# A scheduler's clock with other matmul costs, and a margin before side matmuls, in a two-layer hybrid trunk

## The chip, the cores and the metric

The kernel runs on one core of a Trainium2 chip. The metric is the device time of one execution in microseconds; the time before is the median of three runs. The engines are named as in the profile: PE (TensorE, its weight loads apart as PEld), DVE (VectorE), ACT (ScalarE), POOL (GpSimd) and SP (SyncE).

## The reference, cut to what matters

256 tokens of width 1024 pass two layers. All products are computed in float32 accuracy.

```python
for l in range(2):
    x = x + 0.5 * swiglu_ffn(rms_norm(x, ffn1_norm[l]), ...)        # 1024 -> 2 x 2816 -> 1024
    h = rms_norm(x, mix_norm[l])
    rg_x, rg_g, sb_q, sb_k, sb_v, c_q, c_kv, k_r, gate_logits = jnp.split(h @ w_in[l], ...)
    y_a = rg_lru(causal_depthwise_conv(rg_x, ...), ...) * jax.nn.gelu(rg_g)
    y_b = stick_breaking_attention(sb_q, sb_k, sb_v)                # 8 heads of 128
    y_c = mla_branch(c_q, c_kv, k_r, ...)                           # 8 heads, latents of 256
    g_a, g_b, g_c = jnp.split(jax.nn.sigmoid(gate_logits), 3, axis=-1)
    merged = g_a * (y_a @ w_branch_a[l]) + g_b * (y_b @ w_branch_b[l]) + g_c * (y_c @ w_branch_c[l])
    x = x + merged @ w_out[l]
    x = x + 0.5 * swiglu_ffn(rms_norm(x, ffn2_norm[l]), ...)
return rms_norm(x, final_norm)
```

## The kernel before

The activations stay in SBUF, transposed (features on the partitions). All weights are read once, as one stream of sub-blocks of 128 x 512 floats in the order in which they are used. Each float32 value, of a weight or of an activation, is split into two float32r parts: ACT casts the high part, DVE subtracts it to get the low part. Weights are split in pieces of 1024 columns (`split_to`, line 409), two pieces ahead of their use (tiles `raw`, `hi`, `lo`). A product is then three float32r products. In a feature group (`feature_group`, line 509: 256 features of all tokens) each k-tile of 128 rows gives four matmuls, for each of two blocks one of 512 columns against `hi` and one of 256 columns against `lo`. In a token group (`token_group`, line 530) a k-tile gives six of 512 columns. These groups are the **main stream**. Their sums are in two PSUM tiles `acc`, for short or last groups in `side` tiles, of which there are four.

Between the two feed-forward blocks of a layer stands the mixer, whose groups come in the order `MIX_ORDER` (line 31). What is not a large product there is **side work**: generators that take up a group's result (`evac`), the stick-breaking attention (`stick_pair`, line 907), the recurrence with its gate matmuls (`rg_chain`, line 830, which reads `r` tiles made by ACT and DVE), latent attention (`mla_pair`, line 1061), norms (`squares`, line 612, and `broadcast`, line 642). A group that needs a result of side work asks for it when it comes to that k-tile (`Pairs`, line 1128), and `drain` (line 313) then emits what is missing, whether it fits or not. The branch products ask in this way: `brb` for stick-breaking attention, `bra` for the recurrence, `brc` for latent attention, two k-tiles for each pair of heads.

All engines run their instructions in program order. The order is decided when the program is built, by a model clock (`Clock`, line 120): for each engine the time until which it is held, and for each tile when it was written and read and by which engine. Each instruction is an `Op` (line 156) with a cost in ns by its engine and shape (lines 172 to 186): a DVE operation of n columns costs 68 + 1.042 n as a rule, an ACT operation 95 + 0.833 n, and a matmul 2.5 + 0.4167 n with n at least 256, four times the columns for float32 operands. The clock has no term for one engine's work slowing another's. `Op.emit` (line 191) books the instruction and calls the engine at line 197, so that nearly every instruction stands at L197 in the profile.

Main-stream instructions are emitted at once. After each k-tile of a group, `tick` (line 295) goes through the running tasks and emits the operations at the head of each for as long as `fits` (line 262) allows. For DVE and ACT an operation may start at most 50 ns (500 for urgent tasks, which are those that take up results) after the later of its engine's clock and PE's, and unless urgent must end within 1800 ns of PE's clock. For PE these lines decide, in which `s` is the earliest start by the clock, with 130 ns after a write by another engine:

```python
        if op.e == "pe":
            if s > c.t["pe"] + 60:
                return False
            if not t["urgent"]:
                if self.side <= 0:
                    return False
                self.side -= op.cost
            return True
```

`side` is set to 350 ns at each tick. A task's operations are emitted in its own order, so one that is refused holds back those behind it in its task, and no other task's.

Of the kernel before, what the change touches and what calls it, by code (L numbers as in the profile page):

```python
# [6 lines left out]
F32 = mybir.dt.float32  # L7
# [16 lines left out]
# columns of the packed per-layer vectors  # L24
# [12 lines left out]
# of each group of columns: the matrix, the first column, the k-tiles  # L37
# [9 lines left out]
def group_stream(what, n):  # L47
    """Sub-blocks of [128, 512]: one k-tile of 512 columns, or two k-tiles of 256."""
    if what == "ckv":
        for k in range(0, 9, 3):  # L50
            yield ("ckv0", "in", k, C_C + 256)
            yield ("ckv1", "in", k, C_C + 256)
    elif what in TOKENS:
        m, c, nk = TOKENS[what]
        for k in range(nk):
            yield ("one", m, k, c + 512 * n)
    elif what in FEATURES:
        m, c, nk = FEATURES[what]
        for k in range(0, nk, 2):
            yield ("two", m, k, c + 256 * n)  # L60
    else:
        for k in range(0, KD, 2):
            yield ("gu", what, k, 128 * n)


def layer_stream(l):
    """Order in which a layer's weight sub-blocks of [128, 512] are read."""
    for f in (1, 2):
        if f == 2:
            for g in MIX_ORDER:  # L70
                yield from group_stream(*g)
        for n in range(KF):
            yield from group_stream(f"gu{f}", n)
        if (l, f) == (L - 1, 2):
            for n in range(2):
                yield from group_stream("last", n)
        else:
            for n in range(4):
                yield from group_stream(f"dn{f}", n)
# [10 lines left out]
class Slots:  # L90
    """Tiles handed out in the order in which they were given back."""
# [17 lines left out]
# for each function the tables to load for it; a table holds all functions that name it  # L109
# [10 lines left out]
class Clock:  # L120
    """Estimated times (ns): until when each engine is held by what has been emitted, and
    when each tile's contents are there and have been read."""
# [33 lines left out]
class Op:  # L156
    """An instruction to be emitted, with what it costs by the clock."""

    def __init__(self, engine, name, op, args, kw):
        self.f, self.e, self.args, self.kw = getattr(engine, op), name, args, kw  # L160
        self.engine = engine
        out = kw.get("out", args[0] if args else None)
        n = 1
        for d in out.shape[1:]:
            n *= d
        outs = [out] + ([kw["accum_out"]] if kw.get("accum_out") is not None else [])
        aps = [x for x in (*args, *kw.values()) if hasattr(x, "tensor")]
        self.outs = {x.tensor.name for x in outs}
        self.ins = {x.tensor.name for x in aps if all(x is not o for o in outs)}
        self.table, self.tail = None, 80  # L170
        if op == "dma_start":
            self.cost, self.tail = 50, 2500
        elif name == "pe":
            self.tail = 165
            wide = op == "matmul" and args[2].dtype == F32
            self.cost = 2.5 + 0.4167 * (4 * n if wide else max(n, 256))
        elif name == "act":
            self.table = TABLES.get(kw.get("func"))
            extra = sum(90 for k in ("scale", "bias") if not isinstance(kw.get(k, 0.0), (int, float)))
            self.cost = 95 + extra + 0.833 * n  # L180
        elif name == "dve":
            fast = op in ("tensor_scalar", "tensor_copy") and all(x.space != bass.MemoryType.PSUM for x in aps)
            rate = {"reciprocal": 6.5, "tensor_tensor_scan": 2.1}.get(op, 0.55 if fast else 1.042)
            self.cost = 68 + rate * n
        else:
            self.cost = 150 + (166 if kw.get("op") == ALU.pow else 2.1) * n

# [12 lines left out]
class Timed:  # L200
    """An engine whose instructions are emitted at once from the main stream, and left to
    the scheduler from side work."""
# [15 lines left out]
class Tasks:  # L218
    """Side work: generators whose instructions are emitted, each generator's in order, where
    the clock says that they hold up no engine. What follows a yield runs after what came  # L220
    before it has been emitted."""
# [8 lines left out]
    SIDE = 350  # L230

# [30 lines left out]
    def fits(self, op, t):  # L262
        c = self.clock
        if op.e in ("pool", "sp"):
            return True
        s = op.when(c)
        if op.e == "pe":
            if s > c.t["pe"] + 60:
                return False
            if not t["urgent"]:  # L270
                if self.side <= 0:
                    return False
                self.side -= op.cost
            return True
        if s > max(c.t[op.e], c.t["pe"]) + t["early"]:
            return False
        return t["urgent"] or s + op.cost <= c.t["pe"] + self.LIMIT

    def advance(self, t, force=False):
        """Emits what it can of a task; whether there was any."""  # L280
# [32 lines left out]
    def drain(self, *tasks, done=None):  # L313
        """Emits the given tasks, whether they fit or not, to their end or until `done`."""
# [19 lines left out]
def trunk(tc, xT_in, pos_in, w_in, rgw_in, fin_in, const_in, out):  # L334
# [4 lines left out]
    with ctx:  # L339
# [18 lines left out]
        # x^T, two k-tiles of [128, 256] in each  # L358
# [4 lines left out]
        # [hi | lo] of two k-tiles  # L363
# [27 lines left out]
        def load(out, in_):  # L391
            """One of the first loads: they come one after the other."""
            nc.sync.dma_start(out=out, in_=in_)  # L393
            n = 4 * 128
            for d in out.shape[1:]:
                n *= d
            arrival[0] += max(n / 360, 475)
            clock.written[out.tensor.name] = (arrival[0] + 950, "dma")
# [56 lines left out]
        def both(ap):  # L455
            """[128, 256] as [128, 2, 256]"""
            return ap.rearrange("p (j t) -> p j t", j=1).to_broadcast([128, 2, 256])

        def hilo(src, hl, j=None, g=1.0):
            """src [128, 2, 256], or k-tile j of it, in two float32r parts."""  # L460
# [39 lines left out]
        def parts(a):  # L500
            """What of [128, 2, ...] each tile of a's holds."""
# [7 lines left out]
        def feature_group(kts, evac, last=0):  # L509
            """256 features of all tokens: the two halves of a bank are summed by `evac`. The  # L510
            last steps run block by block."""
# [18 lines left out]
        def token_group(kts, evac, last=0):  # L530
            """512 features, tokens on the partitions."""
# [15 lines left out]
        def narrow_group(kts, width, weights, evac):  # L547
            """The same with [128, width] weights, as (hi, lo) from `weights`."""
# [9 lines left out]
        def features(a):  # L558
            """What a feature group made, to SBUF."""
# [8 lines left out]
        def scaled(a, src, key, extra=None):  # L568
            """The same, times a scale per token."""
# [13 lines left out]
        def transpose_pair(srcs, o):  # L583
            """Two [128, 128] blocks from column o of every token tile, to [128, 2, 256]."""
# [18 lines left out]
        def first_norm(nm, n):  # L603
            """K-tiles 2n and 2n+1 of x are final: their two parts, and squares."""
# [37 lines left out]
        def broadcast(b, r, dst, key, start=False):  # L642
            """Columns r [128, NT], to a row of them on every partition."""
# [10 lines left out]
        class Lazy:  # L654
            """The k-tiles of x^T, each pair asked for when it is needed."""
# [113 lines left out]
        def gen_scaled(a, scales):  # L769
            """PSUM [tok, 512] times a per-token scale, to SBUF; alternating engines."""  # L770
# [40 lines left out]
        def rg_g(mx, p):  # L811
            def gelu(x):
                """x (1 + tanh(c (x + 0.044715 x^3))): twice the gelu."""
# [16 lines left out]
        def rg_chain(mx, ps):  # L830
            """Gates, recurrence and output gate of the channel pairs ps (256 channels each)."""
            vo = mx["v"]
            # with y = -log(a): a = exp(-y), 1 - a^2 = T (1 + a)^2, T = tanh(y / 2)
# [59 lines left out]
        def head_T(mx, key, p, r, extra=None):  # L893
            """Two heads, transposed."""
# [12 lines left out]
        def stick_pair(mx, p):  # L907
# [8 lines left out]
            for j in range(2):  # L916
# [9 lines left out]
                # log(1 + exp(z)) = max(z, 0) + log(1 + exp(-|z|))  # L926
# [72 lines left out]
        def rope(e, dst, src, tmp, nh, t):  # L999
            """dst = src rotated; all [128, nh, 64], tmp [128, nh, 64]."""  # L1000
# [40 lines left out]
        def k_rope(mx, f):  # L1041
            """[tok, 64] in columns t * 256 of f, to [64, tok] on both halves of the partitions,
            with zeros in place of the other half."""
# [84 lines left out]
        class Pairs:  # L1128
            """K-tiles that side work makes, two at a time."""
# [12 lines left out]
        def mix(nm, ntasks, nxt, l):  # L1142
# [37 lines left out]
            def many(work, width):  # L1180
                """Up to `width` at a time, each of them a task that can be waited for."""
# [12 lines left out]
            def gate(b, n):  # L1194
                def sigmoid(f):
                    """1 + tanh(x / 2): twice the sigmoid."""
# [10 lines left out]
            def branch(i, b, n):  # L1207
                """The i-th of the branches."""
# [108 lines left out]
        def tables():  # L1317
            """cos and sin of the positions' angles, and 4 softplus(-lambda)."""
# [144 lines left out]
```

## Time and profile before

| | us |
|---|---|
| median of three runs | 1467.37 |
| lowest and highest run | 1466.5, 1467.78 |
| span of the profiled execution | 1467.2 |
| PE busy | 1442.0 |
| PEld busy | 1261.0 |
| DVE busy | 1115.6 |
| ACT busy | 894.3 |
| POOL busy | 146.1 |

For the profiled execution the page gives its span, from the first to the last instruction; no other time of that execution is recorded, so sums are made against the span. Busy times are unions of the records of an engine. The ends of matmuls are modelled and overlap with the next, so PE's true pace is read from the starts of successive matmuls. In the names, numbers of buffers are left out: `acc<-r,hi` is a main matmul from an activation part and a high weight part, `side<-r,r` a gate matmul, `side<-f,f` a matmul of attention, `side<-f,cst` of 256 columns the broadcast of a norm.

### The profile page before, as it was taken

Reading aid. Unit: us, or ns where it says so; the run is one execution under the profiler, and the core shown is the slowest. Engines: PE = TensorE matmul, PEld = TensorE weight load, DVE = VectorE, ACT = ScalarE, POOL = GpSimd, SP = SyncE. Lnnn points to the kernel's source line nnn. Section 1 sums busy time; section 2 is a strip of 40 time slices with the busy share of each in tenths; the row PEclk is TensorE's granted clock in tenths of the full one; section 3 lists DMA queues with packets and bytes.
Section 4 is the critical chain, followed back from the end, with each engine's and each line's share of the span. In section 5 each row is a group of like instructions: output and inputs, shape, how many; then the busy total and the mean of one; then the engine's idle time right before and its main releaser. Section 6 shows DMA issues by size and latency. Waiting matters only on the chain.

```text
span 1467.2 us, 20804 instructions
## 1 busy us (share of the span) xinstructions
PE 1442.0 (98%) x8248; PEld 1261.0 (86%) x8248; DVE 1115.6 (76%) x1548; ACT 894.3 (61%) x1372; POOL 146.1 (10%) x120
## 2 busy tenths in 40 slices
PE   6999999999999999999999999999999999999998
PEld 5888888888888888888888888898888888888886
DVE  6878567689987788877677766676989877877853
ACT  4665446888665656665455554478885655566643
POOL 3000001123310000000000000111334000100001
PEclk9999999999999999999999999999999999999999
DMA  6555555534543455555545554544445434555452
GB/s 215 199 201 177 197 180 180 179 134 153 182 171 144 145 199 176 197 188 187 200 172 189 184 200 173 187 174 149 151 156 189 169 122 173 195 190 196 179 199 86
DMA packets 38081, 258.15 MB, mean 176 GB/s; under 512 B 4320, under 2 KB 4960, under 8 KB 7520
## 3 DMA queue, kind: packets, MB, share of 16 engines
q1 hardware_dynamic: 37152, 254.21, 48.5%
q0 software_dynamic: 832, 2.62, 0.6%
q8 instruction: 64, 1.05, 0.3%
q14 instruction: 33, 0.27, 0.1%
HBM read 255.77 MB, written 1.05 MB: 175 GB/s over the span
## 4 chain that ended last, share of the span: by engine, by line
PE 92%; DVE 5%; issue 1%; ACT 1%; DMA 0%; SPq 0%; POOLq 0%; POOL 0%; DVEq 0%; ACTq 0%
PE acc L197 77%; PE side L197 15%; DVE lo L197 2%; DVE f L197 2%; DVE r L197 1%; DMA x<-xT 0%; ACT hi L197 0%; ACT f L197 0%; SPq L393 0%; ACT r L197 0%; POOLq L1459 0%; POOL rms L197 0%; DVE rms L197 0%; DVEq L197 0%; ACTq L197 0%
## 5 line engine op out<-in xcount | busy, mean ns | idle before, releaser
L197 PE MATMUL acc<-r,hi 128*128 128x512 f32 x3148 | 1135.1, 403 | 9.4 <-ACT hi L197 5.5
L197 PE MATMUL acc<-r,lo 128*128 128x256 f32 x3148 | 882.7, 280 | 2.1 <-DVE lo L197 2.1
L197 DVE TENSOR_TENSOR lo<-raw,hi 128x1024 fp32r<-128x1024 f32 (+2 forms) x485 | 596.4, 1232 | 235.7 <-ACT hi L197 234.2
L197 PEld LDWEIGHTS acc<-r,hi 128*128 128x128 f32 x3148 | 593.0, 188 | 141.0 <-ACT hi L197 5.5
L197 PEld LDWEIGHTS acc<-r,lo 128*128 128x128 f32 x3148 | 596.7, 190 | 5.6 <-DVE lo L197 3.1
L197 ACT CAST hi<-raw 128x1024 fp32r<-128x1024 f32 (+2 forms) x485 | 501.5, 1040 | 137.3 <-PE acc L197 95.0
L197 POOL TENSOR_TENSOR f<-f,f 128x512 f32<-128x512 f32 (+1 forms) x51 | 89.1, 1753 | 1039.8 <-ACT f L197 955.8
L197 ACT COPY f<-acc 128x512 f32<-128x512 f32 x166 | 97.4, 587 | 126.7 <-PE acc L197 122.9
L197 ACT ACTIVATE f<-f 128x256 f32<-128x256 f32 (+3 forms) x190 | 94.9, 502 | 84.5 <-DVE f L197 83.3
L197 DVE TENSOR_TENSOR f<-acc,f 128x512 f32<-128x512 f32 x166 | 113.8, 685 | 39.1 <-ACT f L197 38.5
L197 DVE TENSOR_TENSOR f<-f,f 128x512 f32<-128x512 f32 x179 | 126.3, 706 | 8.8 <-ACT f L197 2.6
L197 PE MATMUL acc<-hi,r 128*128 128x512 f32 (+2 forms) x344 | 96.9, 358 | 0.0
L197 ACT CAST r<-f 128x256 fp32r<-128x256 f32 (+2 forms) x130 | 58.6, 455 | 61.1 <-DVE f L197 59.8
L197 PE MATMUL side<-r,hi 128*128 128x512 f32 x260 | 92.0, 395 | 0.0
L197 PE MATMUL side<-r,lo 128*128 128x256 f32 x260 | 72.6, 279 | 0.0
L197 PE MATMUL side<-f,f 128*128 128x256 f32 (+1 forms) x320 | 71.6, 327 | 0.0
L197 PEld LDWEIGHTS acc<-hi,r 128*128 128x128 f32 x344 | 61.6, 189 | 8.4
L197 DVE TENSOR_TENSOR r<-f,r 128x256 fp32r<-128x256 f32 (+2 forms) x130 | 64.7, 502 | 2.0 <-ACT r L197 1.9
L197 PE MATMUL acc<-lo,r 128*128 128x512 f32 (+2 forms) x172 | 61.1, 355 | 0.0
L197 PEld LDWEIGHTS side<-r,hi 128*128 128x128 f32 x260 | 48.7, 187 | 11.1
L197 PEld LDWEIGHTS side<-f,f 128*128 128x128 f32 x320 | 45.8, 190 | 4.9
L197 PEld LDWEIGHTS side<-r,lo 128*128 128x128 f32 x260 | 49.1, 189 | 0.0
(89 smaller groups left out, 806.2 us busy)
## 6 DMA issues: line engine op xcount, KB each, us to landing
raw<-w SPq DMA_DIRECT2D x238, 1024.0 KB, 4.8
f<-rgw POOLq DMA_DIRECT2D x8, 256.0 KB, 3.4
raw<-w SPq DMA_DIRECT2D x7, 256.0 KB, 6.9
out<-f SPq DMA_DIRECT2D x4, 256.0 KB, 2.2
x<-xT SPq DMA_DIRECT2D x3, 256.0 KB, 6.7
f<-fin POOLq DMA_DIRECT2D x2, 256.0 KB, 3.7
cst<-const SPq DMA_DIRECT2D x1, 336.0 KB, 5.5
x<-xT SPq DMA_DIRECT2D x2, 128.0 KB, 2.5
```

The costliest lines, as they stand in the source:

```text
L197: return self.f(*self.args, **self.kw)
```

## The change

It does two things. The cost of a PE instruction comes from a new function, `streamed`, which tells transposes, float32, float32r and the rest apart. And a PE operation of side work (or of a norm) is let in only where the modelled end of each operand that another engine wrote lies at least `LATE` = 900 ns before PE's clock. `drain` and forced emission do not ask `fits` and are as before. Everything else in the diff takes out comments.

```diff
@@ class Op
         elif name == "pe":
             self.tail = 165
-            wide = op == "matmul" and args[2].dtype == F32
-            self.cost = 2.5 + 0.4167 * (4 * n if wide else max(n, 256))
+            self.cost = self.streamed(op, args[2].dtype if op == "matmul" else F32, n)
...
+    @staticmethod
+    def streamed(op, dtype, n):
+
+        if op == "transpose":
+            return max(109, 0.852 * n)
+        if dtype == F32:
+            return 2 * max(112, 0.852 * n)
+        if dtype == F32R:
+            return 13.5 + 0.4167 * max(n, 256)
+        return 30 + 0.4167 * n
+
+    def settled(self, c):
+
+        return max((c.written[n][0] for n in self.ins if n in c.written and c.written[n][1] != self.e), default=0.0)
+
@@ class Tasks
     SIDE = 350
+
+    LATE = 900
...
         if op.e == "pe":
             if s > c.t["pe"] + 60:
                 return False
+            if op.settled(c) + self.LATE > c.t["pe"]:
+                return False
             if not t["urgent"]:
```

## Rows read from the trace of the kernel before

**Rows 1.** The page, part 1: busy time of each engine, its share, instructions.
```profile
PE 1442.0 (98%) x8248; PEld 1261.0 (86%) x8248; DVE 1115.6 (76%) x1548; ACT 894.3 (61%) x1372; POOL 146.1 (10%) x120
```
**Rows 2.** The page, part 2: the granted clock of PE in 40 slices.
```profile
PEclk9999999999999999999999999999999999999999
```
**Rows 3.** The chain that ended last: start, length, engine, tile, count.
```profile
31.97 155.31 PE acc L197 x896
...
499.26 25.66 PE acc L197 x148
```
**Rows 4.** Windows: length, then busy time of each engine with its instructions.
```profile
0.00:32.00 32.00, 20.53 (x83) 16.58 (x84) 18.80 (x27) 13.47 (x23) 11.21 (x13) 1.00 0.67 234
1062.00:1068.00 6.00, 3.66 (x23) 3.19 (x24) 6.00 (x8) 5.32 (x9) 3.11 (x3) 1.00 0.44 138
```
**Rows 5.** All waits of PE: total us, times, longest.
```profile
PE acc L197 <- ACT hi L197: 5.5, 1, 5.5
PE side L197 <- DVE r L197: 4.7, 4, 1.5
PE acc L197 <- DVE r L197: 3.9, 1, 3.9
PE acc L197 <- DVE lo L197: 2.1, 2, 1.9
PE side L197 <- DVE f L197: 1.9, 2, 0.9
```
**Rows 6.** Timeline of PE, layer 0: start, length, instruction, and idle before.
```profile
339.22 0.36 PE L197 MATMUL side<-r,r 128*128 128x256 f32 x1
340.48 0.38 PE L197 MATMUL side<-r,r 128*128 128x256 f32 x1 [0.90 <-DVE r L197]
...
341.40 0.65 PE L197 MATMUL side<-r,r 128*128 128x256 f32 x4
341.88 0.40 PE L197 MATMUL acc<-r,hi 128*128 128x512 f32 x1
...
342.57 0.28 PE L197 MATMUL side<-r,r 128*128 128x256 f32 x1
344.32 0.62 PE L197 MATMUL side<-r,r 128*128 128x256 f32 x3 [1.47 <-DVE r L197]
...
406.89 0.28 PE L197 MATMUL acc<-r,lo 128*128 128x256 f32 x1
408.10 0.70 PE L197 MATMUL side<-f,cst 128*128 128x256 f32 x2 [0.93 <-DVE f L197]
```
**Rows 7.** Timelines of DVE and of POOL at these places.
```profile
340.35 1.63 DVE L197 TENSOR_TENSOR lo<-raw,hi 128x1024 fp32r<-128x1024 f32 x1
341.90 2.37 DVE L197 TENSOR_TENSOR r<-f,r 128x512 fp32r<-128x512 f32 x2
...
406.21 1.83 DVE L197 TENSOR_SCALAR f<-cst,rc 128x128 f32<-128x128 f32 x2
...
340.99 2.13 POOL L197 TENSOR_TENSOR f<-f,f 128x512 f32<-128x512 f32 x1
...
405.15 2.28 POOL L197 TENSOR_TENSOR f<-f,f 128x512 f32<-128x512 f32 x1
```
**Rows 8.** Windows as in rows 4; the third busy time is that of DVE.
```profile
310.00:320.00 10.00, 10.00 (x64) 8.96 (x63) 9.96 (x17) 8.70 (x16) 3.24 (x3) 1.00 0.44 141
...
340.00:350.00 10.00, 8.05 (x50) 7.13 (x51) 9.97 (x10) 6.80 (x12) 7.49 (x5) 1.00 0.32 107
```
**Rows 9.** Timelines: a split on DVE, and PE's first matmul on its result.
```profile
294.81 1.23 DVE L197 TENSOR_TENSOR lo<-raw,hi 128x1024 fp32r<-128x1024 f32 x1 [3.33 <-ACT hi L197]
...
296.80 0.28 PE L197 MATMUL acc<-r,lo 128*128 128x256 f32 x1
```
**Rows 10.** Timelines: the last attention matmul of layer 0, and a result's two parts.
```profile
498.87 0.38 PE L197 MATMUL side<-f,f 128*128 128x128 f32 x2
...
340.32 0.58 ACT L197 CAST r<-side 128x512 fp32r<-128x512 f32 x1
...
344.19 0.68 DVE L197 TENSOR_TENSOR r<-side,r 128x512 fp32r<-128x512 f32 x1
```

## The prediction

> **What bounds the kernel now.** I read the busy shares first: PE is busy 1442.0 us of a span of 1467.2, DVE 76% and ACT 61% [rows 1]. The slices say that this holds in every stretch, and that the granted clock is at full speed nearly throughout [rows 2]. Since matmuls overlap in such records, I checked the stream by start-to-start times: in the first feed-forward 896 matmuls take 155.31 us with no gap, 0.347 us per pair of one 512- and one 256-column matmul [rows 3]. So the kernel is a dense stream of matmuls, and only two things could shorten it without removing a matmul: the head, where PE is busy 20.53 of the first 32 us [rows 4], and the few places where PE waits. The change adds, removes and resizes no instruction; it only reorders. The whole prize is therefore in the list of PE's waits [rows 5]. Its three entries at `acc` belong to the head, before the side work of the mixers; those at `side` are 4.7 + 1.9 = 6.6 us.
>
> The timeline shows these six: three in each layer, at the same places, so I work them out in layer 0 and double. The gate matmuls of `rg_chain` (`side<-r,r`) stand 0.12 us apart when nothing is late (four in 0.48 us); one stands 1.26 us after its forerunner and another 1.75: stalls of 1.14 and 1.63 us. The broadcast of the latent norm (`side<-f,cst`) starts 1.21 us after a 256-column matmul that takes 0.12: a stall of 1.09 [rows 6]. That is 3.86 us per layer, **7.7 us in all** (6.6 as the wait view counts it, which starts from modelled ends). A window of layer 1 shows the same hole: 3.66 us busy of 6.00 [rows 4].
>
> **Why PE waits there.** In program order PE runs everything in turn, so a side matmul put in too early holds up the whole stream behind it. The clock thought that the operand was there; DVE was late. Behind 340 us two `r<-f,r` took 2.37 us together where the clock has 0.60 for each (68 + 1.042 x 512 ns), and a `lo` split took 1.63 where it has 1.14, while POOL ran a 2.13 us tensor_tensor; before the broadcast, two DVE operations of 128 columns took 1.83 us, beside a POOL operation of 2.28 us [rows 7]. The clock knows nothing of this; nothing in its costs couples POOL with DVE.
>
> **The change, part by part.** (1) *The margin.* So far a side matmul was let in when its operand's modelled time plus 130 was at most PE's clock plus 60, that is 70 ns behind it. Now 900 ns are wanted: 830 more. Side work is tried once per tick, every four matmuls or 0.69 us in a feature group, so an operation slips by one tick or two (0.69 or 1.39), 0.83 on average. If DVE's lag stays as it is, the isolated stall of 1.09 falls by 0.83. The two gate stalls are one lag of 1.14 + 1.63 = 2.77, which also falls by 0.83 alone. Gain 1.66 per layer, **3.3 us** in all: the lower bound. The upper bound is all of it, **7.7**, since the new order also shifts which DVE operation meets which POOL operation, and a lag of the usual size (around 1.1 twice in three) is nearly covered by 0.83. I take the middle, 5.5 us: the two isolated stalls argue for the upper end, the double one for the lower.
>
> (2) *The PE costs.* An f32r pair was 215.8 + 109.2 = 325.0 ns in the clock, and is now 226.9 + 120.2 = 347.1; 448 pairs make 145.6 and 155.5 us, and the trace has 155.31 [rows 3]. So PE's clock was 6.8% fast, and that worked as a hidden margin: within one period DVE really had 6.8% more time than the clock gave it. That margin goes away. Where side work fills DVE (9.96 and 9.97 us busy of 10 in the first and the last slice from 310 to 350 [rows 8]), the clock now lets in up to 6.8% more: at most 2.7 us of extra lag over 40 us. It can hit two things: the side matmuls of part 1, and the `lo` splits of the weights. The thinnest `lo` in the mixer is done at 296.04 and used at 296.80: 0.76 us [rows 9]. So bounds of 0 and, for each layer, 2.7 us; I take 0.5 per layer, **1.0 us** lost in all, near zero because that split comes after 3.33 us of idle DVE and so carries no accumulated lag. The other forms (f32 matmuls of 256 columns 429 to 436, transposes 109 to 109) change by too little to count. The one-column matmuls of `squares` go from 4 to 224 ns each in the clock, four times a norm, ahead of a broadcast that doesn't wait today: zero.
>
> (3) *What is late next.* Every side chain now takes longer, by a tick or two at each step from ACT or DVE to PE. Behind a held-back matmul stand only its own task's later operations; the main stream passes it. Cover is the distance to the group that needs the result. For latent attention that is thinnest: the last value matmul starts at 498.87 [rows 10], and `brc0` (the first of the 128 matmuls that end the run of 148 [rows 3]) starts at 499.26 + 20 x 0.173 = 502.7, needing that last pair at its k-tile 6, 24 matmuls or 4.2 us later: 506.9. In between lie the two parts of the result, an ACT cast of 0.58 and a DVE subtraction of 0.68 [rows 10]. Slack: 506.9 - 498.9 - 0.4 - 1.3 = 6.3 us. Zero while fewer than some seven steps of 0.83 add up on the chain. The stick-breaking and rg-lru chains have been done for tens of us when they are needed. Urgent matmuls (norms, latents) slip too: a tick or two, hidden by PSUM banks that need no rb to come free. (4) *Table loads* on ACT may change in number with the order; ACT has room (61%) and PE waits for it only in the head [rows 5]: zero. The head has hardly any side matmuls: unchanged, 0.5 us either way.
>
> **Sum:** 1467.2 - 5.5 + 1.0 = 1462.7 for the span of the profiled execution; the median of the runs lies 0.17 above that span, so **1462.9 us**.
>
> A page of the Trainium skill speaks against part 2. "TensorE: Matmul & The Clock Gate", section "Wait — 56ns, not 53.3ns?", gives a warm matmul N / 2.4 + 2.5 ns: just the old formula, by which 448 pairs would take 145.6 us and the new clock would be the wrong one. The trace disagrees with it here, with 155.31.
>
> **Rivals.** *A: the lags form anew.* DVE meets POOL elsewhere, and one operation is held for a whole POOL instruction: 2.28 us [rows 7]. Less 0.83 that leaves 1.45 a time; three times in two layers make 8.7 in place of 7.7: 1467.2 + 1.0 = 1468.2, **no change**. For it: two of the three stalls of a layer have a POOL operation of over 2 us beside them. Against: most of the lags seen are near 1.1. The skill's page "SBUF — State Buffer", section "SBUF: two separate sides", states it as a lock of a port shared by DVE and GpSimd, where the loser waits for the whole instruction; the stretched rows agree. *B: DVE is overfilled, slower.* The honest PE clock lets more side work onto a DVE that is already full. Place: 310 to 350 and 380 to 427 in each layer; price: 6.8% of 40 and 47 us, 2.7 and 3.2 us of lag, less the margin of 0.83, as new waits: 4.2 per layer, 8.5 in all, on top of the old stalls less 3.3: 1467.2 + 8.5 - 3.3 = **1472.4**. It decides from an added lag of about 2.3 us. For it: full DVE windows [rows 8]; against: if DVE were the clock's limit in them, a clock that counts 1.14 us for a split of 1.23 [rows 9] would have lost more than three stalls by now. *C: latent attention is late for `brc0`.* Nine steps at 1.1 us make 9.9, 3.6 over the slack, 7.2 in two layers: 1462.9 + 7.2 = **1470.1**. *D: the margin never binds* at these six, because they were forced: none is emitted by a drain of its group, so little for it; then 1467.2.
>
> **Chances.** Forecast 55%, A and D 25%, B 12%, C 8% (half of it beyond the bound). 0.2% is 2.9 us, what a measurement of this kernel can tell from no change: faster below 1464.4, slower above 1470.3. B's smaller sizes count as no change. Faster 0.54, same 0.29, slower 0.17. The range goes from all stalls gone and a little of the head, 1459.0, to near B, 1471.0.
>
> **What would show it.** Right: PE's waits on the side fall from 6.6 us to about 2; pairs still 0.347 us; PE busy time nearly the same; the last value matmul of latent attention 2 to 4 us later against `brc0`. Part 2 wrong: new waits `acc <- DVE lo` in the mixers. A: `side <- DVE` waits of the old total at other places, each beside a POOL operation. C: a PE wait just before or in `brc`. The forecast is wrong if the side waits vanish and the span does not follow, or if PE waits of over 1 us turn up in the main stream.

## The result and the profile after

The changed kernel takes 1477.75 us (median of four runs, 1476.9 to 1481.33) against 1466.93 for the kernel before: the ratio is 1.0079, with a 95% interval of 1.0066 to 1.0092. The forecast was 1462.9 us, faster, with a range to 1471.0. The change made the kernel slower by 0.8%.

The page of the changed kernel, the lines that answer to [rows 1, 2] and the shares of the chain that ended last:

```profile
PE 1446.3 (98%) x8248; PEld 1262.5 (86%) x8248; DVE 1113.8 (76%) x1548; ACT 889.8 (60%) x1372; POOL 136.2 (9%) x120
...
PEclk9999999999999999999999999999999999999999
...
PE 76%; ACT 11%; DVE 9%; issue 3%; POOL 0%; DMA 0%; SPq 0%; POOLq 0%; DVEq 0%; ACTq 0%
```

and the last of them in the kernel before:

```profile
PE 92%; DVE 5%; issue 1%; ACT 1%; DMA 0%; SPq 0%; POOLq 0%; POOL 0%; DVEq 0%; ACTq 0%
```

The same instructions in the same number: nothing here tells where 10.8 us went, except that 11% of the chain is now ACT, in place of 1%, and 9% DVE, in place of 5%. The waits of PE do, beside [rows 5]:

```profile
PE acc L211 <- DVE f L211: 6.4, 2, 3.2
PE acc L211 <- ACT hi L211: 5.5, 1, 5.5
PE acc L211 <- DVE lo L211: 3.1, 4, 1.9
PE acc L211 <- DVE r L211: 2.6, 1, 2.6
PE side L211 <- DVE r L211: 2.6, 4, 0.9
PE side L211 <- DVE f L211: 0.7, 2, 0.4
PE side L211 <- DVE lo L211: 0.2, 1, 0.2
```

The side waits that the margin was to shorten did fall, from 6.6 to 3.5 us. A new wait of the **main stream** took their place, `acc <- DVE f`, once in each layer. The timeline of PE shows it at the group `ckv0`, which needs one of the two `acc` banks:

```profile
387.58 0.28 PE L211 MATMUL acc<-r,lo 128*128 128x256 f32 x1
391.07 0.63 PE L211 MATMUL acc<-hi,r 128*128 128x320 f32 x1 [3.21 <-DVE f L211]
391.50 0.47 PE L211 MATMUL acc<-lo,r 128*128 128x320 f32 x1
391.77 0.73 PE L211 MATMUL acc<-hi,r 128*128 128x320 f32 x2
392.30 0.47 PE L211 MATMUL acc<-lo,r 128*128 128x320 f32 x1
392.57 0.73 PE L211 MATMUL acc<-hi,r 128*128 128x320 f32 x2
...
395.40 0.46 PE L211 MATMUL acc<-hi,r 128*128 128x320 f32 x2
395.70 0.31 PE L211 MATMUL acc<-lo,r 128*128 128x320 f32 x1
395.85 0.46 PE L211 MATMUL acc<-hi,r 128*128 128x320 f32 x2
```

The windows there (columns as in [rows 4], the granted clock third from the end) show what follows the wait:

```profile
385.00:390.00 5.00, 2.86 (x17) 2.21 (x15) 5.00 (x4) 2.54 (x3) 4.33 (x4) 1.00 0.01 3
390.00:395.00 5.00, 3.93 (x18) 3.93 (x19) 4.96 (x9) 0.00 (x0) 0.20 (x1) 0.66 0.56 210
```

PE stood still for 3.2 us, and behind it the granted clock is 0.66 on the mean of five microseconds: nine of the first 320-column matmuls take three for 0.80 us (391.77 to 392.57 in the timeline), later ones three for 0.45 (395.40 to 395.85). So they ran at 1.2 GHz in place of 2.4. By start times the wait costs 3.4 us and the slow stretch 1.4 us; in layer 1 it is 3.4 and 1.6. That is 9.8 us for both layers.

Why was the bank not free? `branch` takes it up in two steps, an ACT copy and a DVE addition. The timelines of ACT, DVE and POOL in the changed kernel:

```profile
382.25 0.59 ACT L211 COPY f<-acc 128x512 f32<-128x512 f32 x1 [1.29 <-PE acc L211]
...
382.73 1.76 DVE L211 TENSOR_TENSOR lo<-raw,hi 128x1024 fp32r<-128x1024 f32 x1
384.41 1.22 DVE L211 SCALAR_TENSOR_TENSOR f<-f,f 128x512 f32<-128x512 f32 x1
385.56 0.96 DVE L211 TENSOR_TENSOR f<-f,cs 128x256 f32<-128x256 f32 x1
386.44 1.77 DVE L211 SCALAR_TENSOR_TENSOR f<-f,f 128x512 f32<-128x512 f32 x1
388.13 2.28 DVE L211 TENSOR_TENSOR lo<-raw,hi 128x1024 fp32r<-128x1024 f32 x1
390.34 0.68 DVE L211 TENSOR_TENSOR f<-acc,f 128x512 f32<-128x512 f32 x1
...
383.37 5.96 POOL L211 TENSOR_TENSOR f<-f,f 128x256 f32<-128x256 f32 x4
```

The copy was done at 382.84; the addition started 7.5 us later. Three side operations and two weight splits stand ahead of it on DVE, 7.99 us of records where the clock has 0.60, 0.33, 0.60 and twice 1.14, that is 3.81; POOL ran its rotary operations beside nearly all of them. In the kernel before the same addition follows one split, and is done 2.2 us before `ckv0` starts at 388.77:

```profile
384.17 1.76 DVE L197 TENSOR_TENSOR lo<-raw,hi 128x1024 fp32r<-128x1024 f32 x1
385.85 0.68 DVE L197 TENSOR_TENSOR f<-acc,f 128x512 f32<-128x512 f32 x1
```

The stream was short of prepared weights already. A piece of weights is split two pieces ahead, and between 345 and 380 us its low part was ready 3.1 us before use on the mean in the kernel before, and 0.45 us in the changed one (first use of each piece less the end of its split, from the two traces). At one piece of each layer PE waited for it, here with the split that it waited for:

```profile
352.39 1.34 DVE L211 TENSOR_TENSOR lo<-raw,hi 128x1024 fp32r<-128x1024 f32 x1 [0.91 <-ACT hi L211]
...
353.78 0.39 PE L211 MATMUL acc<-r,lo 128*128 128x256 f32 x1 [0.48 <-DVE lo L211]
```

The split itself waited for ACT, and that holds for the stretch: the high parts, which ACT casts, were ready 5.1 us before use in the kernel before and 2.2 us in the changed one, and a split began 0.5 us after its high part in both. DVE had room there and ACT had none, as a window of the changed kernel and the same one of the kernel before show (the third busy time is that of DVE, the fourth that of ACT):

```profile
360.00:370.00 10.00, 10.00 (x57) 8.47 (x56) 7.40 (x10) 9.94 (x17) 2.16 (x2) 1.00 0.58 212
...
360.00:370.00 10.00, 10.00 (x59) 8.64 (x58) 8.71 (x12) 9.91 (x18) 0.00 (x0) 1.00 0.64 217
```

So up to 380 us it was ACT's casts that came late. DVE fell behind only from there on: its split at 378.60 began 0.4 us after the high part was ready, the one at 388.13 more than 7 us after.

To compare parts of whole kernels I take, from each trace, the start of every matmul less the sum of the new formula's costs of those before it: what is left over is time lost on PE. The stretches are 203 to 430 and 925 to 1152 us, the first 227 us of each mixer; the mixers go on to 562 and 1284.

| us lost on PE | 203 to 430 | 925 to 1152 | both |
|---|---|---|---|
| before | 5.6 | 5.9 | 11.6 |
| after | 11.4 | 11.4 | 22.9 |
| new costs, no margin | 15.8 | 14.3 | 30.1 |
| old costs, margin 900 | 5.3 | 6.4 | 11.7 |
| new costs, margin, DVE x 1.068 | 5.3 | 5.2 | 10.5 |
| new costs, margin, ACT x 1.068 | 9.9 | 9.8 | 19.7 |
| float32r cost old, margin | 9.1 | 9.2 | 18.2 |
| float32r cost new alone, margin | 14.1 | 14.9 | 29.0 |
| old costs, margin 450 | 3.2 | 3.1 | 6.3 |

After less before is 11.3 us: the loss is in the mixers. That the medians differ by nearly the same, 10.8, is in part chance. Counted in the same way, the changed kernel loses 2.7 us more than the kernel before in the rest of the mixers, and in the trace of the kernel before 3.2 us are lost in the first feed-forward of layer 1, at a slower pace (last section), and 2.3 us more in the head; the spans of the two traces differ by 7.9 us.

### The profile page after: what moved, and what is told of

Its sections match the earlier page's. It is cut to its first block, busy times and chain, and to the rows that moved or that the text cites. A ratio compares the mean times of both kernels' runs of the same rounds, so it can differ in the third digit from the quotient of the medians.

```text
span 1475.1 us, 20791 instructions
## 1 busy us (share of the span) xinstructions
PE 1446.3 (98%) x8248; PEld 1262.5 (86%) x8248; DVE 1113.8 (76%) x1548; ACT 889.8 (60%) x1372; POOL 136.2 (9%) x120
## 4 chain that ended last, share of the span: by engine, by line
PE 76%; ACT 11%; DVE 9%; issue 3%; POOL 0%; DMA 0%; SPq 0%; POOLq 0%; DVEq 0%; ACTq 0%
PE acc L211 64%; PE side L211 12%; ACT f L211 5%; DVE f L211 4%; DVE lo L211 4%; ACT hi L211 3%; ACT L132 2%; DVE r L211 1%; ACT r L211 1%; POOL f L211 0%; DMA x<-xT 0%; SPq L411 0%; POOLq L1477 0%; POOL rms L211 0%; DVE rms L211 0%
## 5 line engine op out<-in xcount | busy, mean ns | idle before, releaser
L211 POOL TENSOR_TENSOR f<-f,f 128x512 f32<-128x512 f32 (+1 forms) x51 | 81.5, 1606 | 983.1 <-ACT f L211 954.5
L211 DVE TENSOR_TENSOR f<-f,f 128x512 f32<-128x512 f32 x179 | 123.0, 689 | 10.9 <-ACT f L211 4.6
L211 PE MATMUL acc<-hi,r 128*128 128x512 f32 (+2 forms) x344 | 103.6, 372 | 6.4 <-DVE f L211 6.4
```

Source lines behind the costliest of these rows:

```text
L211: return self.f(*self.args, **self.kw)
```

## The experiments

All ratios are to the kernel before on the same chip, with 95% intervals.

**Which half of the change: new costs alone, margin alone.**

```diff
-            if op.settled(c) + self.LATE > c.t["pe"]:
-                return False
```

> The changed kernel with its new PE costs and without the margin of 900 ns. Overfill theory (the honest PE clock lets 6.8% more side work onto DVE, so that the bank for the first ckv group comes free late): the wait of about 3.4 us at that group stays in both layers, and the side waits of the kernel before (7.7 us by start times) come back or grow: 1476 to 1484 us. Margin theory (it is the 900 ns that shift the rotary work onto that place): no wait there, 1463 to 1469 us.

1483.08 us, 1.0113 (1.0092 to 1.0134).

```diff
-            self.cost = self.streamed(op, args[2].dtype if op == "matmul" else F32, n)
+            wide = op == "matmul" and args[2].dtype == F32
+            self.cost = 2.5 + 0.4167 * (4 * n if wide else max(n, 256))
```

> The changed kernel with the old PE costs and with the margin of 900 ns. Overfill theory: no wait at the first ckv group, the side waits fall from 7.7 to 2 to 4 us: 1461 to 1466 us. Margin theory: the wait at ckv stays, 1474 to 1479 us.

1468.35 us, 1.0007 (0.9997 to 1.0016): no change. The new costs are the harm: 16 us without the margin, 9 with it. The time with them is as the overfill theory said, but not the place: without the margin the waits are spread, and none is at `ckv`. Waits of PE with the new costs alone:

```profile
PE side L211 <- DVE f L211: 6.7, 4, 2.1
PE side L211 <- DVE r L211: 6.5, 8, 1.6
...
PE acc L211 <- DVE lo L211: 5.4, 6, 1.9
```

and with the margin alone:

```profile
PE side L212 <- DVE f L212: 4.1, 2, 2.2
PE acc L212 <- DVE r L212: 3.9, 3, 2.5
PE acc L212 <- DVE lo L212: 3.6, 4, 1.9
```

With the margin alone the gate and broadcast stalls of [rows 6] are gone, and PE loses 0.5 us between 203 and 345 in place of 3.2. The gain is given back: 3.9 us (layer 1: 5.5, with a slow stretch of the clock) between 345 and 380 in place of 0.5, most of it where the `uqr` group waits for a `side` bank that DVE has not yet read, 2.2 us in layer 0 and 1.9 in layer 1. So the expected 2 to 4 us of side waits was met in size, and the time was not.

**Is it POOL?** The rotary operations of the first token tile go to DVE.

```diff
-                    rope((gp, dve)[t], ...)
+                    rope((dve, dve)[t], ...)
```

> The changed kernel with the six rotary operations of the first token tile (10.2 us on POOL just ahead of the ckv group) on DVE, where the other token tile's are, at about 0.35 us each. Collision theory (DVE is late because these POOL operations stretch its own): the wait of 3.4 us and the 1.4 us that the lower clock costs behind it go in both layers, 9.6 us less: 1467 to 1470 us. Overfill without POOL (DVE has too much work there whatever POOL does): DVE gets 2 us more, the wait grows to about 5 us: 1479 to 1483 us.

1481.56 us, 1.0101 (1.0086 to 1.0116). The collision theory as put falls: the time rose. The wait for the bank did shrink, to 1.8 us as the waits show from 6.4 in the changed kernel, so POOL had a part in its size. But between 380 and 430 us the kernel loses 6.8 us, against 6.3 in the changed one, now in other waits, and the low parts are as late as there between 345 and 380.

```profile
PE side L211 <- DVE f L211: 6.7, 5, 1.7
...
PE acc L211 <- DVE lo L211: 4.7, 9, 1.9
...
PE acc L211 <- DVE f L211: 1.8, 2, 0.9
```

**Is it the ratio of the clock's PE to its DVE?**

```diff
-            self.cost = 68 + rate * n
+            self.cost = 1.068 * (68 + rate * n)
```

> The changed kernel with all DVE costs of the clock times 1.068, which gives back the old ratio of DVE to PE and keeps the honest PE costs and the margin. Overfill theory: the wait at the first ckv group goes or falls below 1 us: 1464 to 1470 us. If the ratio of the two clocks has nothing to do with it: 1475 to 1480 us.

1468.82 us, 1.0012 (1.0002 to 1.0022): 9 us better than the changed kernel by one factor in DVE's cost. The low parts of the weights are ready 2.3 us early between 345 and 380, in place of 0.45, and the high parts 4.9 in place of 2.2, so the factor on DVE gave ACT time too. The wait at `ckv` is gone, and PE waits on the side for 4.3 us:

```profile
PE side L211 <- DVE f L211: 3.5, 4, 1.0
...
PE side L211 <- ACT f L211: 0.8, 2, 0.6
```

**Does the ratio explain all?** ACT is scaled too, and the margin taken out; then the booking limit halved; then both engines dearer still.

```diff
-            self.cost = 95 + extra + 0.833 * n
+            self.cost = 1.068 * (95 + extra + 0.833 * n)
-            self.cost = 68 + rate * n
+            self.cost = 1.068 * (68 + rate * n)
-            if op.settled(c) + self.LATE > c.t["pe"]:
-                return False
```

> New PE costs, no margin, and the clock's DVE and ACT costs both times 1.068. Ratio theory (what hurts in the new PE costs is only that the other two engines look 6.8% less loaded against PE than before): the order is nearly that of the kernel before, 1465 to 1470 us, against 1483 for the new costs and no margin. If it is another part of the new costs (the dearer one-column and small float32 matmuls, the cheaper bf16 ones): it stays at 1477 to 1484 us.

1497.94 us, 1.0213 (1.0195 to 1.0231).

```diff
-    LIMIT = 1800
+    LIMIT = 900
```

> The changed kernel with side work of ACT and DVE booked at most 900 ns ahead of PE's clock in place of 1800. Overfill theory: ACT and DVE come out less far behind, the wait at the first ckv group falls below 1.5 us and the low parts of the weights are again ready over 1 us early between 345 and 380 us: 1465 to 1472 us. If the booking limit is not what lets the work in (it is let in by operands that are ready): 1475 to 1479 us.

1487.1 us, 1.0142 (1.0125 to 1.016).

```diff
-            self.cost = 95 + extra + 0.833 * n
+            self.cost = 1.068 * (95 + extra + 0.833 * n)
-            self.cost = 68 + rate * n
+            self.cost = 1.15 * (68 + rate * n)
```

> The changed kernel with DVE costs times 1.15 and ACT costs times 1.068, so that the clock fills both engines less than the kernel before did. Overfill theory: fewer and smaller waits in the mixers than with DVE times 1.068 alone (5.3 us per layer by start times against 5.6 before): 1458 to 1466 us. If side work now comes too late for the groups that need it, it is emitted by force: waits in front of brb0, ukv0 or brc0, 1468 to 1480 us.

1511.17 us, 1.0301 (1.0282 to 1.0321). The ratio theory in its strict form falls: the order is not that of the kernel before. What the three share is the other side of the same balance. The low parts are 4.7, 3.4 and 6.7 us early between 345 and 380. But side work is late, and groups force it. In the order that the scheduler makes, no matmul of the kernel before or of the changed kernel is forced; in these three kernels matmuls of the stick-breaking attention are. It is not `brb0` that calls for them: a `uq` group wants two of the four `side` tiles (`small_banks`), fewer are free, and `wait` emits what holds the others. Waits of PE of the first of the three, and the largest one in its timeline, inside a `bra` group, whose next operand `r` is a product of the recurrence:

```profile
PE acc L211 <- DVE r L211: 15.3, 3, 5.9
...
PE side L211 <- ACT r L211: 5.5, 4, 2.6
```
```profile
465.03 0.79 PE L211 MATMUL acc<-r,hi 128*128 128x512 f32 x1 [5.94 <-DVE r L211]
```

**Which of the new costs?** First float32r back to the old cost, all else new; then the reverse.

```diff
         if dtype == F32R:
-            return 13.5 + 0.4167 * max(n, 256)
+            return 2.5 + 0.4167 * max(n, 256)
```

> The changed kernel with the old cost of float32r matmuls (2.5 ns + columns) and the new costs of all other forms, with the margin. If the 6.8% on the main stream are what hurts: as with all old costs and the margin, 1465 to 1471 us. If the small forms are (one-column matmuls 4 to 224 ns, bf16 masks 109 to 57 and 83): 1475 to 1480 us.

1470.66 us, 1.0027 (1.0016 to 1.0037).

```diff
+        if op == "matmul" and dtype == F32R:
+            return 13.5 + 0.4167 * max(n, 256)
+        wide = op == "matmul" and dtype == F32
+        return 2.5 + 0.4167 * (4 * n if wide else max(n, 256))
```

> The changed kernel with the new cost of float32r matmuls and the old costs of all other forms, with the margin. If the 6.8% on the main stream hurt: 1474 to 1482 us, with the low parts of the weights less than 1 us early on the mean between 345 and 380 us. If the small forms do: 1465 to 1471 us.

1482.39 us, 1.0105 (1.0088 to 1.0122). The float32r cost is what hurts most, 12 us between the two. The small forms cost little in time, 1.0027 against 1.0007 with the margin alone, though they change the order: with them PE loses 18.2 us in the stretches of the table, against 11.7 with the margin alone, and waits 1.4 and 2.7 us a layer at the short `uq` groups. The sign is in the waits: with the new float32r cost the main stream waits for low parts (two waits of the head are in this row of every kernel, 2.1 us before) and for banks,

```profile
PE acc L208 <- DVE lo L208: 7.2, 9, 2.7
...
PE acc L208 <- DVE f L208: 3.8, 6, 0.8
```

and with the old one neither. The place I had named for it was not met: with the new float32r cost alone the low parts are 2.5 us early between 345 and 380, not under 1; the thin stretch is 380 to 430, with 1.5 us on the mean and one piece 1.1 us late.

**The margin: 450 ns at old costs, 1800 at new.**

> The kernel before with a margin of 450 ns and nothing else. If the side waits of the kernel before shrink with the margin and the new waits with 900 ns (3.9 and 5.5 us between the rg gates and brb0) come from side work that is late, half the margin loses less there: 1461 to 1466 us. If each order has waits of its own that no margin of this size steers: 1465 to 1472 us, at places that neither neighbour has.

1464.86 us, 0.998 (0.9971 to 0.999): faster than both kernels, the one order that is. One of its ten runs took 3699.76 us, and the ratio is without it. One stall a layer is left beside the head:

```profile
PE acc L212 <- DVE r L212: 3.3, 1, 3.3
PE acc L212 <- DVE lo L212: 2.1, 2, 1.9
PE side L212 <- DVE r L212: 1.5, 2, 0.8
```

> The changed kernel with twice the margin, 1800 ns. If the lag of DVE and ACT behind the clock is what the margin has to cover, and the margin also slows the side work that fills them: 1468 to 1476 us, with smaller side waits. If the waits of the changed kernel are those of the main stream (weights, banks), which the margin does not guard: 1475 to 1485 us, with latent attention later against brc0.

1480.94 us, 1.0094 (1.0079 to 1.0109): as the second theory had it. Stick-breaking matmuls are now forced, ahead of the `uq0` group and for its `side` tiles, two waits of 5.3 us, and the main stream still waits for a bank, 2.8 us a layer, at 414 us:

```profile
PE side L211 <- ACT r L211: 10.7, 2, 5.3
PE acc L211 <- DVE f L211: 5.6, 2, 2.8
```

**What makes side work late, and is 450 ns a trend?**

```diff
-            self.cost = 95 + extra + 0.833 * n
+            self.cost = 1.068 * (95 + extra + 0.833 * n)
```

> The changed kernel with ACT costs times 1.068 alone, margin kept. If ACT's cost is what makes side work late (its chains of exp, ln and table loads no longer fit): waits of side work in front of brb0 and bra0, 1485 to 1505 us. If ACT is overfilled as DVE is: the waits of the changed kernel shrink, 1467 to 1475 us.

1476.17 us, 1.006 (1.0045 to 1.0075): neither. The time is that of the changed kernel, but the waits are others. The wait at `ckv` is gone and the low parts are 2.5 us early between 345 and 380, just as with the factor on DVE; yet PE loses 19.7 us in the stretches of the table, 1.8 us a layer of it for a `side` bank at 375 us. So to take these two signs away is not enough to get the time back.

> The changed kernel with DVE costs times 1.068 and without the margin. If the margin is worth what it is worth at the new costs (5 us): 1472 to 1477 us. If the missing margin was what made side work late with both engines dearer: 1485 us or more. If DVE's ratio alone sets it and the margin does nothing: 1467 to 1471 us.

1484.42 us, 1.0114 (1.0099 to 1.0129). Between the first two expectations: without the margin, side work is late again and forced by a `uq` group (`side <- ACT r` 9.5 us, longest 4.7). The margin is worth 16 us there.

> The kernel before with a margin of 300 ns. Trend (the margin takes away side waits until it makes side work late): between 0 and 450 ns, 1465 to 1467 us. Luck of one order: anywhere from 1462 to 1472 us.

1482.53 us, 1.0109 (1.0088 to 1.0129).

> The kernel before with a margin of 600 ns. Trend: between 450 and 900 ns, 1465 to 1468 us, with the three stalls of a layer at 0 to 1 us in all and waits from late side work below 3 us a layer. Luck of one order: anywhere from 1462 to 1472 us.

1468.42 us, 1.001 (0.9999 to 1.002). There is no trend: at old costs, margins of 300, 450, 600 and 900 ns give 1482.5, 1464.9, 1468.4 and 1468.4 us. With 300 the waits are at other places: 2.85 us at 387 us for a `side` bank that DVE had not yet read, and 2.0 us at 510 us for an operand `r` of the main stream. The gain at 450 is that order's luck as far as these runs show.

**A second trace of the kernel before.**

> The kernel before once more, for a second trace. In its first trace the first feed-forward of layer 1 runs at 0.353 us per pair of matmuls and all others at 0.347, which is 3.1 us over that stage. If the pace belongs to the program (its addresses and its order), the same stage is slow again; if it belongs to the execution, another stage or none is.

1466.77 us, and the same stage is slow again; but see the last section.

## Why the prediction was wrong

**What bounds the kernel** stood: no instruction changed, PE's waits decide, the loss is in the mixers. It left out what follows a wait: 3.0 us of the loss are the two slow stretches behind the waits at `ckv`. The sign that it named for being wrong came, a wait of over 1 us in the main stream.

**Part 1, the margin.** Predicted: 3.3 to 7.7 us gained. The stalls of [rows 6] did go, and the side waits fell to 3.5 us in the changed kernel. The step that failed is that the gain was taken as lasting. Between 203 and 345 us the changed kernel loses 3.3 us, as the kernel before does (3.2), 1.1 of it now at a stick-breaking matmul at 301. Alone, the margin removes 2.7 us before 345 and loses 3.4 between 345 and 380 in layer 0, and the time does not move (1.0007). Rival A said in kind that the lags form anew; it put them at side matmuls beside POOL, and they formed at `side` banks. A hold of a whole POOL instruction is not the rule either: of the 57 weight splits that ran beside a POOL operation in the kernel before, half take the usual 1.23 us or less, and the longest 2.32.

**Part 2, the PE costs.** This is the term that decided, and it was mis-sized by about ten times: 1.0 us lost was taken, between bounds of 0 and 5.4 for both layers; the costs lost 16 us alone and 9 with the margin. The mechanism was named, a clock that was 6.8% fast and so hid lag. Two steps failed. The lag was expected to hit side matmuls and splits; the largest loss was at the **release of a bank**, 9.8 us at `ckv`, where the addition that frees `acc` waits behind every operation that the clock let in ahead of it on DVE. And "near zero because that split comes after idle DVE" looked at one thin place of the old order, and at DVE alone: between 345 and 380 the high parts of ACT came late, and DVE, which had room there, waited for them. Rival B had this direction and the right second place (380 to 427), at a chance of 12%, but with 1472.4 us half of the loss: its 4.2 us per layer were for two places, where `ckv` alone cost 4.8 to 5.0. Its first place did not occur, with DVE busy 31.7 of the 40 us from 310 to 350, in place of 39.8. It was lowered by the argument that an overfull DVE would have shown more stalls before. That it showed none because the fast PE clock kept it from being overfull fits the runs, but no run shows it by itself.

**The Trainium skill's formula** for a warm matmul ("TensorE: Matmul & The Clock Gate", section "Wait — 56ns, not 53.3ns?") equals the old cost, and the trace still disagrees: the first feed-forward takes 155.31 us for 896 matmuls in the changed kernel too. The truer cost gave the slower kernel.

**Part 3.** Latent attention was not late for `brc0` in the changed kernel. At other settings late side work was a main loss, in `bra`, which I had thought covered by tens of us, and at `uq` groups, which need no result of it but two of the `side` tiles that it holds, a call that the prediction did not see.

**Rivals C and D** did not occur.

What is not settled: why one order is better than another at equal costs. Every kernel with the new float32r cost and no other engine dearer lies at 1477 to 1487 us, and five of six with the old one (the kernel before among them) at 1465 to 1471; the sixth, with 300 ns, at 1482.5. That the changed kernel has its weights ready less early and frees a bank late is shown, and what that cost; with one factor on DVE both are undone and the time is back, with one on ACT both are undone and it is not. That the new cost must do so in any order is not shown.

## What to carry to other kernels

When a schedule is made by a model clock, its errors can hold each other up: making one engine's cost true while the others stay optimistic can take away a margin that nobody wrote down. To scale the others along is no recipe either: a factor of 1.068 on DVE gave the time back, on ACT it did not, and on both without the margin the kernel took 1497.94 us (both with the margin was not run). Judge by what the main stream waits for (banks to be freed, operands prepared ahead), not by the stalls that the change was aimed at. Ask also which engine prepares them: a late DVE can be a late ACT. And where orders with nearly equal settings differ by 15 us, time several of them before reading a trend into one.

## What the runs showed of the hardware that was not expected

A wait of PE of 3.2 us cost 1.4 to 1.6 us more behind it, at a granted clock that fell to half; the stalls of 1.1 to 1.6 us of [rows 6] cost nothing of that kind. The length of the wait alone does not decide it: with the margin alone, five microseconds behind the `uqr` wait the granted clock is 1.00 in layer 0 (wait of 2.2 us) and 0.66 in layer 1 (1.9 us), and behind the waits of 2.85 us with 300 ns it is 1.00.

The first feed-forward of a layer runs at one of two paces, 0.347 or 0.353 us per pair of matmuls, at a granted clock of 1.00 in both, and holds it through the stage, about 3 us apart. The slower one stands also behind 500 us in the changed kernel's mixer. In the kernel before it is the slow one in layer 1, in both traces. But the changed kernel and the one with the rotary work on DVE have the same order on PE, ACT and DVE in the first feed-forward, and the chain that ended last has there, in this sequence of kernels,

```profile
29.64 155.31 PE acc L211 x896
```
```profile
30.86 158.29 PE acc L211 x896
```

so the order of the instructions up to there does not set it. What does is open; a single trace can be 3 us off for it, and differences of that size between two spans mean little.
